# Attention stage of a decoder trunk: TensorE's order pinned as traced, projections dealt anew, look-ahead of seven tiles

## Chip, cores and metric

One core of one Trainium2 chip. The metric is device time in microseconds of one execution, median of 3 runs.

## The reference

One layer: a modulated RMSNorm, one input projection, an RWKV-7 group (8 heads x 64) and a stick-breaking attention group (8 heads x 64), gates, an output projection and a final norm, for 2048 tokens of 1024 features in float32. The change touches the attention group and the projections that run beside it:

```python
def block(args):
    q_blk, idx = args
    z = einsum('bhqd,bhkd->bhqk', q_blk, k) * scale
    log_1m = where(mask, log_sigmoid(-z), 0.0)
    after = cumsum(log_1m, axis=3, reverse=True) - log_1m
    attn = where(mask, exp(log_sigmoid(z) + after), 0.0)
    return einsum('bhqk,bhkd->bhqd', attn, v)
```

So each weight is sigmoid(z) times the product of sigmoid(-z) over all later keys, then the weights are summed with V.

## The kernel before

Three stages follow each other: an early one (modulation, normed input, first projections), the attention stage, and the RWKV stage with the output projection. The first two share a scheduler, which sets each engine's order from a simulated timeline of its own; RWKV has another.

The attention stage has 16 steps n = 4j + b: head pair j of four, block b of four of 512 tokens. Step b has 8(b + 1) tiles of 128 queries by up to 512 keys, since only earlier keys count. `seq` lists all tiles. For one tile, `scores` makes two TensorE matmuls into a PSUM tile `z` (high and low part of the queries in `qt` against the keys in `kt`), ScalarE takes two sigmoids (`u`, `s`), VectorE scans `u` from the last key to the first, and GpSimd multiplies `s` by it. `turn` transposes one key block of the four tiles of a group into the PSUM tile `tr`; ScalarE copies it (`ah`) and VectorE takes the difference (`al`), which together hold the full precision. `weigh` makes two matmuls of V with `ah` and `al`, summed in the one PSUM tile `av`. `attend` calls `scores` for the tile LEAD places ahead, then `turn`, then `weigh` for the tile LAG places behind. At a step's end `finish` transposes the result (`otp`), norms it and stores it in DRAM.

Beside it, `fill` makes the projections that later steps need: K, Q and V of a step (`proj_k`, `proj_q`, `proj_v`) and the gates (`proj_g`, kinds g and r, one for each block), each 24 matmuls of 512 columns (V: 96 of 128 columns) into a PSUM tile `mm`, from weights split by `w_split`. After a Q projection ScalarE copies (L419), VectorE takes the low part (L420) and three DMAs spread it over the partitions (L422 to L424); the third writes what the first two read, so it comes after them. `combine` fetches a finished output, transposes it and multiplies it by its gate. `_merge` interleaves `attend` and `fill` by their estimated work (`fill_work`), and this gives the traced order; the scheduler then chooses its own.

PSUM has eight banks: one `mm`, three `z`, two `tr` (also used by `otp`, `wtp` of `w_split` and `combine`), one `av`, one for a mask. A projection is bound to the last sum traced before it (`pace`) from step 12 on.

Of the kernel before, what the change touches and what calls it, by code (L numbers as in the profile page):

```python
# [18 lines left out]
P = 128  # L19
D = 1024  # L20
KB = D // P
# [67 lines left out]
def trunk(nc, a, out):  # L89
# [22 lines left out]

    NM = [1, 3, 2]
    early = [True]

    def mm_ps(name="mm"):
        if early[0]:
            return z_ps(name)
        return pp.tile([P, TB], F32, tag="mm", bufs=NM[0], name=name)

# [95 lines left out]
    for e in range(2):  # L216
        mrow = [f("mrow") for f in ((z_ps, z_ps) if e == 0 else (z_ps, av_ps))]
        for k in range(KB):
            ad = ada_rows(e, k)
            for i in range(2):  # L220
                PE.matmul(mrow[i][0:1], cact[:, k:k + 1], ad[:, i * TB:(i + 1) * TB], start=k == 0, stop=k == KB - 1)
        if e == 0:
            load_x(0)
        modr = xp_.tile([P, D], F32, tag="macc", bufs=2, name="modr")
        for i in range(2):
            A.activation(out=modr[0:1, i * TB:(i + 1) * TB], in_=mrow[i][0:1], func=AF.Copy)
        for m in range(8):
            PE.matmul(mod[:, 8 * e + m:8 * e + m + 1], modr[0:1, m * P:(m + 1) * P], ones[0:1, 0:1],
                      start=True, stop=True)
# [95 lines left out]
    def w_split(kind, j):  # L325
# [4 lines left out]
        dg = wl.rearrange("p k c -> p (k c)")[:, 0:2 * P].bitcast(F32)  # L330
        A.activation(out=dg, in_=ident, func=AF.Copy, scale=m1)
        tp = tr_ps("wtp")
        PE.matmul(tp[:, 0:P], ones, dg, start=True, stop=True)
# [28 lines left out]

    pace = [None]

    def inproj(w, b, name):
        wh, wl = w[0], w[1]
        ps = mm_ps(name)
        for k in range(KB):
            with tc.issue_after(pace[0]) if pace[0] is not None else nullcontext():
                PE.matmul(ps, wh[:, k], hth[b][:, k], start=k == 0, stop=False)  # L370
            PE.matmul(ps, wh[:, k], htl[b][:, k], start=False, stop=False)  # L371
            PE.matmul(ps, wl[:, k], hth[b][:, k], start=False, stop=k == KB - 1)  # L372
            yield 0.65
        return ps

    def inproj_tok(w, b, name):
        wh, wl = w[0], w[1]
        ps = mm_ps(name)
        for i in range(4):
            t = slice(i * P, (i + 1) * P)  # L380
            for k in range(KB):
                PE.matmul(ps[:, t], hth[b][:, k, t], wh[:, k], start=k == 0, stop=False)
                PE.matmul(ps[:, t], hth[b][:, k, t], wl[:, k], start=False, stop=False)
                PE.matmul(ps[:, t], htl[b][:, k, t], wh[:, k], start=False, stop=k == KB - 1)
                if k % 4 == 3:
                    yield 0.65
# [74 lines left out]
    def combine(j, b, pool):  # L461
# [9 lines left out]
        DMA.dma_start(out=sg, in_=ydram[4 + j][b])  # L471
        yield 0.45
        tp = tr_ps()
# [6 lines left out]

    NS, NU, LEAD, LAG = 8, 5, 5, 3

# [12 lines left out]
    def scores(n, i, sb):  # L495
# [9 lines left out]
        z = z_ps()  # L505
        PE.matmul(z[:, 0:nk], qt[:, h, 0, qs], kt[:, h, 0:nk], start=True, stop=False)  # L506
        PE.matmul(z[:, 0:nk], qt[:, h, 1, qs], kt[:, h, 0:nk], start=False, stop=True)  # L507
        u = sb.tile([P, TB + 1], F32, tag="u", bufs=NU, name="u")
# [19 lines left out]
    def turn(n, i, sb):  # L528
# [5 lines left out]
        for q in range(q0, 4):  # L534
            PE.transpose(tp[:, q * P:(q + 1) * P], att[gi, q][:, ks * P:(ks + 1) * P], ident)  # L535
        r = slice(q0 * P, TB)
# [6 lines left out]
    def weigh(sb, n, i, ah, al, r):  # L543
# [8 lines left out]
        vs = vst[NB * j + kb][:, ks, h].rearrange("p l d -> p (l d)")  # L552
        PE.matmul(av[:, r], vs, ah[:, r], start=first, stop=False, skip_group_check=True)  # L553
        ins = PE.matmul(av[:, r], vs, al[:, r], start=False, stop=last, skip_group_check=True)  # L554
        if n >= 12:
            pace[0] = ins.ins
        if last:
# [29 lines left out]
    def attend(n, sb):  # L587

        p0 = seq.index((n, 0))
        p1 = p0 + 8 * (n % NB + 1)  # L590
        ahead = LEAD if n % NB else 0
        if n % NB == 1 or n == 0:
            for p in range(p0, p0 + LEAD):
                yield scores(*seq[p], sb)
        for p in range(p0, p1):
            if p + LEAD < min(p1 + ahead, len(seq)):
                yield scores(*seq[p + LEAD], sb)
# [39 lines left out]
    _merge((make_hs(*range(2, NB)), 3.6 * (NB - 2)), (proj_qkv(1), 15.6), (w_split("g", 0), 0.3))  # L637
    gate_row()
    xctx.close()
    cz = [zero1]  # L640
# [6 lines left out]
    def fill(n, sb):  # L647

        j, b = divmod(n, NB)
        end = j == NB - 1  # L650
        if n < 2:
            m = n + 2
        else:
            m = n + 1 if 2 < n < NST - 1 else None
        new = b == 3 and not end
        if b == 0 and j > 0:
            yield from w_split("g", j)
        if b == 2:
            yield from w_split("r", j)
            w_load("z" if end else "k", 0 if end else j + 1)  # L660
        if b == 3:
            yield from w_split("z" if end else "k", 0 if end else j + 1)
            w_load("rk" if end else "q", 0 if end else j + 1)
        gates = [("g", 0)], [("g", 1)], [("g", 2), ("g", 3), ("r", 0)], [("r", 1), ("r", 2), ("r", 3)]
        gates = [proj_g(kind, j, gb, sb) for kind, gb in gates[b]]
        if m is not None:
            yield from proj_k(m)
            if new:
                yield from gates.pop(0)
                yield from w_split("q", j + 1)  # L670
                w_load("v", j + 1)
            yield from proj_q(m)
            if new:
                yield from gates.pop(0)
                yield from w_split("v", j + 1)
                w_load("g", j + 1)
            yield from proj_v(m)
        if j > 0:
            yield from combine(j - 1, b, sb)
        if n == NST - 1:  # L680
            for i in range(4):
                yield from proj_z(i, sb)
                if gates:
                    yield from gates.pop(0)
                if i < 3:
                    yield from w_split(("rk", "rr", "rv")[i], 0)
                if i < 2:
                    w_load(("rr", "rv")[i], 0)
        for g in gates:
            yield from g  # L690
        if b == 1:
            w_load("r", j)

    def fill_work(n):
        b = n % NB
        if n == NST - 1:
            return 5.2 * 7 + 1.5
        return 5.2 * ((4, 4, 6, 6)[b] - 3 * (n == 2)) + 0.9 * (n > 3) + (0.2, 0, 0.2, 0.6)[b]

    dts = []  # L700
    early[0] = False
    with tc.tile_pool(name="sb", bufs=2) as sb:
# [7 lines left out]
        for n in range(NST):  # L710
            b = n % NB
            _merge((attend(n, sb), 8.6 + 10.48 * b), (fill(n, sb), fill_work(n)))
            if n == 1:
# [3 lines left out]
                for i in range(2):  # L717
                    dts.append(dram(f"dt{i}", [2, 2, 8, 65, 64]))
                    for m in range(2):
                        for h in range(2):  # L720
                            DMA.dma_start(out=dts[i][m, h].rearrange("c s t -> s c t")[0:64],
                                          in_=zeros[0:64].rearrange("p (c d) -> p c d", c=8))
    sbk.close()
    pace[0] = None

# [610 lines left out]
```

## Time and profile before

| | |
|---|---|
| median of 3 runs | 1914.78 us (1912.62 to 1915.76) |
| profiled execution | 1910.53 us |
| its span, first to last instruction | 1908.8 us |
| attention stage in it | 129.8 to 1035.8 us |

A row of the timeline gives start, duration, engine, line, operation, what is written from what, shape and count; in brackets the idle time before it and who ended it. Matmuls are pipelined, and a record lasts longer than the distance to the next start. The stretch view gives busy time of each engine, with counts, the granted share of TensorE's clock, and DMA share and rate.

### The profile page before, as it was taken

What the parts mean: (1) busy time and instruction counts of PE and PEld (TensorE: products, weight loads), DVE (VectorE), ACT (ScalarE), POOL (GpSimd) and SP (SyncE); (2) the same over time, 40 slices, a digit from 0 to 9 for tenths busy, and PEclk for the clock granted to TensorE, in tenths of its full rate; (3) what the DMA queues carried; (4) which work ended last, traced back from release to release, by engine and by line L of the source; (5) the groups of instructions that cost most, each with busy time, mean ns of one, the idle gap of its engine ahead of it and who ended that gap; (6) DMA issues with size and microseconds to landing.
All of it is one profiled execution on the core that took longest, in us unless ns stands there. A gap on an engine that the chain in (4) does not pass through costs nothing. (4 is left out here: it accounts for less than half of the span.)

```text
span 1908.8 us, 38922 instructions
## 1 busy us (share of the span) xinstructions
PE 1719.8 (90%) x14880; PEld 1161.5 (61%) x14880; DVE 1348.7 (71%) x2855; ACT 870.0 (46%) x1718; POOL 754.6 (40%) x1106
## 2 busy tenths in 40 slices
PE   7979889999899998999997898898899888989998
PEld 2646556666566665667654455665555565667886
DVE  4876788577776778768775667877877777775542
ACT  2665567366654656546654333323332333422221
POOL 1425466355643646445444223222223232223322
PEclk9889999999999999999998899999999999999999
DMA  8442201222123221132111423222333333236442
GB/s 298 150 116 56 56 26 50 64 64 70 37 56 81 67 56 42 51 92 67 45 50 56 133 55 83 68 60 74 77 81 81 80 77 107 75 94 179 149 138 89
DMA packets 210408, 159.93 MB, mean 84 GB/s; under 512 B 113247, under 2 KB 171820, under 8 KB 210222
## 3 DMA queue, kind: packets, MB, share of 16 engines
q1 hardware_dynamic: 209220, 155.31, 29.2%
q8 instruction: 117, 1.92, 0.4%
q10 hardware_dynamic: 1002, 2.13, 0.4%
q14 instruction: 69, 0.57, 0.1%
HBM read 94.48 MB, written 44.04 MB: 73 GB/s over the span
## 5 line engine op out<-in xcount | busy, mean ns | idle before, releaser
L523 POOL TENSOR_TENSOR s<-s,u 128x512 f32<-128x512 f32 (+2 forms) x320 | 305.8, 963 | 216.5 <-ACT s L511 102.0
L540 DVE TENSOR_TENSOR al<-tr,ah 128x512 fp32r<-128x512 f32 (+1 forms) x320 | 187.4, 599 | 96.3 <-ACT ah L539 95.7
L522 DVE TENSOR_TENSOR_SCAN u<-u,dmask 128x512 f32<-128x512 f32 x192 | 240.0, 1268 | 13.0 <-ACT u L510 11.4
L539 ACT ACTIVATE ah<-tr 128x512 fp32r<-128x512 f32 (+1 forms) x320 | 171.7, 553 | 103.7 <-PE tr L535 99.6
L510 ACT ACTIVATE u<-z 128x512 f32<-128x512 f32 (+2 forms) x320 | 173.4, 555 | 73.4 <-PE z L507 49.0
L535 PE MATMUL tr<-kept_ident,s 128*128 128x128 f32 x1088 | 173.5, 279 | 33.1 <-DVE al L540 26.5
L511 ACT ACTIVATE s<-z 128x512 f32<-128x512 f32 (+2 forms) x320 | 166.2, 549 | 53.0 <-PE tr L535 53.0
L535 PEld LDWEIGHTS tr<-kept_ident,s 128*128 128x128 f32 x1088 | 130.3, 143 | 74.9 <-DVE al L540 38.4
L370 PE MATMUL pss<-kept_hh,kept_wh 128*128 128x512 f16 x416 | 161.3, 388 | 8.8 <-PEq L730 8.8
L372 PE MATMUL pss<-kept_hh,kept_wl 128*128 128x512 f16 x416 | 160.9, 387 | 0.0
L371 PE MATMUL pss<-kept_hl,kept_wh 128*128 128x512 f16 x416 | 160.9, 387 | 0.0
L372 PEld LDWEIGHTS <-kept_wl 128*128 128x128 f16 x928 | 93.2, 100 | 104.9 <-issue 14.2
L370 PEld LDWEIGHTS <-kept_wh 128*128 128x128 f16 x928 | 94.3, 102 | 101.4 <-issue 29.2
L371 PEld LDWEIGHTS <-kept_wh 128*128 128x128 f16 x928 | 93.0, 100 | 94.8 <-issue 25.0
L506 PE MATMUL z<-kt,qt 128*128 128x512 f32 (+2 forms) x320 | 132.1, 417 | 9.5 <-issue 3.7
L553 PE MATMUL av<-ah,vt 128*128 128x512 f32 (+1 forms) x320 | 136.5, 427 | 3.9 <-DVE o L564 2.3
L554 PE MATMUL av<-al,vt 128*128 128x512 f32 (+1 forms) x320 | 136.0, 426 | 0.2 <-DVE al L540 0.2
L507 PE MATMUL z<-kt,qt 128*128 128x512 f32 (+2 forms) x320 | 117.5, 371 | 0.0
L519 DVE TENSOR_TENSOR_SCAN u<-u,dmask 128x128 f32<-128x128 f32 (+3 forms) x128 | 107.3, 867 | 11.6 <-ACT u L510 6.6
L370 PE MATMUL psg<-kept_hh,kept_wh 128*128 128x512 f16 x256 | 99.1, 387 | 10.9 <-DVE klo L434 4.8
L1274 PE MATMUL po<-kept_woh,kept_yh 128*128 128x512 f32 x256 | 102.3, 400 | 0.0
L1275 PE MATMUL po<-kept_wol,kept_yh 128*128 128x512 f32 x256 | 101.5, 397 | 0.0
(296 smaller groups left out, 4146.1 us busy)
## 6 DMA issues: line engine op xcount, KB each, us to landing
kept_raw<-in_w_in SPq DMA_DIRECT2D x29, 512.0 KB, 4.3
ad<-in_ada_w SPq DMA_DIRECT2D x24, 512.0 KB, 5.6
qt<-qt SPq DMA_DIRECT2D x48, 256.0 KB, 3.3
xt<-in_x SPq DMA_DIRECT2D x16, 512.0 KB, 5.1
y<-sg SPq DMA_DIRECT2D x32, 256.0 KB, 2.3
t<-dt SPq DMA_DIRECT2D x64, 128.0 KB, 3.2
xr<-in_x SPq DMA_DIRECT2D x16, 512.0 KB, 3.6
out<-xr SPq DMA_DIRECT2D x16, 512.0 KB, 2.6
```

The costliest lines, as they stand in the source:

```text
L370: PE.matmul(ps, wh[:, k], hth[b][:, k], start=k == 0, stop=False)
L371: PE.matmul(ps, wh[:, k], htl[b][:, k], start=False, stop=False)
L372: PE.matmul(ps, wl[:, k], hth[b][:, k], start=False, stop=k == KB - 1)
L510: A.activation(out=u[:, 0:nk], in_=z[:, 0:nk], func=AF.Sigmoid, scale=-0.125)
L511: A.activation(out=s[:, 0:nk], in_=z[:, 0:nk], func=AF.Sigmoid, scale=0.125)
L522: V.tensor_tensor_scan(out=ur, data0=ur, data1=mr, initial=u[:, nk:nk + 1], op0=ALU.mult, op1=ALU.bypass)
L523: G.tensor_tensor(out=s[:, 0:nk], in0=s[:, 0:nk], in1=u[:, 1:nk + 1], op=ALU.mult)
L535: PE.transpose(tp[:, q * P:(q + 1) * P], att[gi, q][:, ks * P:(ks + 1) * P], ident)
L539: A.activation(out=ah[:, r], in_=tp[:, r], func=AF.Copy)
L540: V.tensor_tensor(out=al[:, r], in0=tp[:, r], in1=ah[:, r].bitcast(F32), op=ALU.subtract)
L553: PE.matmul(av[:, r], vs, ah[:, r], start=first, stop=False, skip_group_check=True)
L554: ins = PE.matmul(av[:, r], vs, al[:, r], start=False, stop=last, skip_group_check=True)
```

## The change

TensorE's matmuls of scores, transposes, sums and projections in the attention stage are chained in the order in which they are traced (`pin`, `pinned`). PSUM has two `mm`, two `z`, two `tr` buffers. The look-ahead is seven tiles and goes on over the ends of steps, the sums are one tile behind. `s` and `u` have 11 and 6 buffers. The projections of the four steps of a head pair are dealt 3, 4, 6, 7 (before 4, 4, 6, 6) and in another sequence. `w_split` and `combine` hand over more often.

```diff
-    NM = [1, 3, 2]
-    early = [True]
+    NM = [2, 2, 2]
     def mm_ps(name="mm"):
-        if early[0]:
-            return z_ps(name)
         return pp.tile([P, TB], F32, tag="mm", bufs=NM[0], name=name)
...
-        mrow = [f("mrow") for f in ((z_ps, z_ps) if e == 0 else (z_ps, av_ps))]
+        mrow = [f("mrow") for f in ((z_ps, z_ps) if e == 0 else (mm_ps, mm_ps))]
...
         A.activation(out=dg, in_=ident, func=AF.Copy, scale=m1)
+        yield 0.3
         tp = tr_ps("wtp")
...
-    pace = [None]
+    order = []
+    def pin(ins):
+        order.append(ins.ins)
+    def pinned():
+        for p, i in zip(order, order[1:]):
+            tc.add_manual_dep(i, p.name, mybir.DependencyInfo(mybir.DependencyClass.NoSync,
+                                                              mybir.DependencyReason.DATA), reason="order")
+        order.clear()
...
-            with tc.issue_after(pace[0]) if pace[0] is not None else nullcontext():
-                PE.matmul(ps, wh[:, k], hth[b][:, k], start=k == 0, stop=False)
-            PE.matmul(ps, wh[:, k], htl[b][:, k], start=False, stop=False)
-            PE.matmul(ps, wl[:, k], hth[b][:, k], start=False, stop=k == KB - 1)
+            pin(PE.matmul(ps, wh[:, k], hth[b][:, k], start=k == 0, stop=False))
+            pin(PE.matmul(ps, wh[:, k], htl[b][:, k], start=False, stop=False))
+            pin(PE.matmul(ps, wl[:, k], hth[b][:, k], start=False, stop=k == KB - 1))
...
-        yield 0.45
+        for _ in range(1 if pool is None else 3):
+            yield 0.8
         tp = tr_ps()
...
-    NS, NU, LEAD, LAG = 8, 5, 5, 3
+    NS, NU, LEAD, LAG = 11, 6, 7, 1
...
-        ahead = LEAD if n % NB else 0
-        if n % NB == 1 or n == 0:
+        if n == 0:
             for p in range(p0, p0 + LEAD):
                 yield scores(*seq[p], sb)
         for p in range(p0, p1):
-            if p + LEAD < min(p1 + ahead, len(seq)):
+            if p + LEAD < len(seq):
+                while seq[p + LEAD][0] not in qst:
+                    yield 0.02
                 yield scores(*seq[p + LEAD], sb)
```

The new `fill`, its core:

```python
def g(kind, gb):
    return proj_g(kind, j, gb, sb)
def kqv(m):
    yield from proj_k(m)
    yield from proj_q(m)
    yield from proj_v(m)
if b == 0:
    ...
    yield from kqv(n + 1 if j > 0 else 2)
if b == 1:
    yield from kqv(n + 1 if j > 0 else 3)
    yield from g("g", 2 if j > 0 else 3)
if b == 2:
    ...
    if j > 0:
        yield from kqv(n + 1)
    yield from g("g", 3 if j > 0 else 2)
    yield from g("r", 3)
    yield from g("r", 2)
if b == 3 and not end:
    ...
    yield from g("g", 1)
    ...
    yield from proj_k(n + 1)
    ...
    yield from proj_q(n + 1)
    yield from proj_v(n + 1)
    yield from g("g", 0)
    yield from g("r", 0)
    yield from g("r", 1)
```

The order that results, at two places. First TensorE at the change from step 4 to step 5, before: from the last Q matmuls of step 5 (`psq`) to the start of its V projection (`psv`, 96 matmuls).

```order
L372 MATMUL psq<-kept_hh_510,kept_wl_288 128x512
L553 MATMUL av<-ah,vt 128x512
L554 MATMUL av<-al,vt 128x512
L553 MATMUL av<-ah,vt 128x384
L554 MATMUL av<-al,vt 128x384
L553 MATMUL av<-ah,vt 128x256
L554 MATMUL av<-al,vt 128x256
L535 MATMUL tr<-kept_ident_61,s 128x128 x4
L553 MATMUL av<-ah,vt 128x128
L535 MATMUL tr<-kept_ident_61,s 128x128 x3
L554 MATMUL av<-al,vt 128x128
L382 LDWEIGHTS kept_hh_510
```

Eight sums and seven transposes stand here; the 96 V matmuls and two more transposes follow, and then the first scores of step 5. Now, the same engine, from the end of the twelfth V matmul behind the last Q matmul:

```order
L392 LDWEIGHTS kept_hl_511
L392 MATMUL psv<-kept_wh_313,kept_hl_511 128x128
L515 MATMUL z<-kt,qt 128x128
L516 MATMUL z<-kt,qt 128x128
L544 MATMUL tr<-kept_ident_61,s 128x128 x3
L390 LDWEIGHTS kept_hh_510
L390 MATMUL psv<-kept_wh_313,kept_hh_510 128x128
```

The first scores of step 5 now stand behind 12 V matmuls, with the remaining 84 and three transposes behind them. K and Q of step 5 (48 matmuls) stand ahead, with one pair of sums, one tile's transposes and the `otp` of step 3 among them.

Second, TensorE in the middle of a long step (step 6), before, at the end of one gate projection (`psg`) and the start of the next:

```order
L506 MATMUL z<-kt,qt 128x512
L507 MATMUL z<-kt,qt 128x512
L506 MATMUL z<-kt,qt 128x512
L507 MATMUL z<-kt,qt 128x512
L535 MATMUL tr<-kept_ident_61,s 128x128 x4
L506 MATMUL z<-kt,qt 128x512
L507 MATMUL z<-kt,qt 128x512
L553 MATMUL av<-ah,vt 128x512
L535 MATMUL tr<-kept_ident_61,s 128x128 x3
L554 MATMUL av<-al,vt 128x512
L370 LDWEIGHTS kept_wh_822
L370 MATMUL psg<-kept_hh_1011,kept_wh_822 128x512
```

Here three tiles' scores, two tiles' transposes and a sum stand together, and 14 projection matmuls follow in a row. Now, within a Q projection of step 5:

```order
L515 MATMUL z<-kt,qt 128x512
L516 MATMUL z<-kt,qt 128x512
L378 LDWEIGHTS kept_wh_287
L378 MATMUL psq<-kept_hh_806,kept_wh_287 128x512
L379 LDWEIGHTS kept_wh_287
L379 MATMUL psq<-kept_hl_807,kept_wh_287 128x512
L380 LDWEIGHTS kept_wl_288
L380 MATMUL psq<-kept_hh_806,kept_wl_288 128x512
L544 MATMUL tr<-kept_ident_61,s 128x128 x4
L562 MATMUL av<-ah,vt 128x512
L563 MATMUL av<-al,vt 128x512
```

One tile's scores, three or six projection matmuls, one tile's transposes and the sums of the tile before it now alternate.

## Rows read from the trace of the kernel before

**Rows 1.** Stretch view: steps 4 and 7, then the whole attention stage.

```profile
core 0: us, PE busy (x) PEld busy (x) DVE busy (x) ACT busy (x) POOL busy (x), PEclk, DMA share, GB/s
359.30:389.80 30.50, 28.37 (x216) 19.71 (x214) 16.05 (x27) 14.03 (x33) 11.95 (x24) 0.94 0.30 79
...
495.40:589.50 94.10, 84.67 (x511) 56.59 (x510) 71.82 (x107) 51.96 (x106) 45.68 (x79) 0.97 0.20 57
...
129.80:1035.80 906.00, 833.70 (x5352) 569.63 (x5352) 678.79 (x1007) 535.92 (x1125) 469.72 (x836) 0.98 0.21 56
```

**Rows 2.** Stretch view of line L371 alone, then of L383 alone, attention stage.

```profile
129.80:1035.80 906.00, 189.53 (x496) 48.92 (x496) 0.98 0.21 56
...
129.80:1035.80 906.00, 77.84 (x448) 43.81 (x448) 0.98 0.21 56
```

**Rows 3.** Costliest groups, TensorE: count, busy us, mean ns, idle before and its releasers.

```profile
L535 PE MATMUL tr<-kept_ident,s 128*128 128x128 f32 x1088 | 173.5, 279 | 33.1 <-DVE al L540 26.5
...
L506 PE MATMUL z<-kt,qt 128*128 128x512 f32 (+2 forms) x320 | 132.1, 417 | 9.5 <-issue 3.7
```

**Rows 4.** Timeline of TensorE in step 7: start us, duration, engine, line, operation.

```profile
563.74 0.22 PE L383 MATMUL psv<-kept_wl,kept_hh 128*128 128x128 f16 x1
563.79 0.22 PE L384 MATMUL psv<-kept_wh,kept_hl 128*128 128x128 f16 x1
...
571.05 0.38 PE L372 MATMUL psg<-kept_hh,kept_wl 128*128 128x512 f16 x1
571.26 1.04 PE L535 MATMUL tr<-kept_ident,s 128*128 128x128 f32 x8
572.06 0.47 PE L553 MATMUL av<-ah,vt 128*128 128x512 f32 x1
572.37 0.40 PE L554 MATMUL av<-al,vt 128*128 128x512 f32 x1
572.61 0.39 PE L370 MATMUL psg<-kept_hh,kept_wh 128*128 128x512 f16 x1
...
575.68 0.39 PE L506 MATMUL z<-kt,qt 128*128 128x512 f32 x1
575.91 0.40 PE L507 MATMUL z<-kt,qt 128*128 128x512 f32 x1
576.15 0.39 PE L370 MATMUL psk<-kept_hh,kept_wh 128*128 128x512 f16 x1
```

**Rows 5.** Waits of TensorE, attention stage: who waited for whom, total us, times, longest.

```profile
PE tr L535 <- DVE al L540: 26.5, 27, 2.2
PE psq L370 <- DVE klo L434: 5.2, 3, 1.7
...
PE psg L370 <- DVE klo L434: 4.8, 3, 2.1
PE z L506 <- issue: 3.7, 2, 1.8
...
PE psg L370 <- DVE sg L456: 3.3, 1, 3.3
PE psg L370 <- DVE z L403: 2.6, 1, 2.6
...
PE z L506 <- DMA qt<-qt: 1.9, 1, 1.9
```

**Rows 6.** Timeline of TensorE, step 4 to 5; last, the view of tile `qt`.

```profile
359.91 0.38 PE L372 MATMUL psq<-kept_hh,kept_wl 128*128 128x512 f16 x1
...
370.10 0.30 PE L506 MATMUL z<-kt,qt 128*128 128x128 f32 x1 [1.83 <-issue]
...
DMA to landing us min/median/max: 2.8/3.3/4.5
```

**Rows 7.** Stretch view, five microseconds behind that wait.

```profile
371.00:376.00 5.00, 5.00 (x17) 1.98 (x17) 2.70 (x4) 2.25 (x7) 3.24 (x9) 0.66 0.19 56
```

**Rows 8.** Costliest groups: VectorE's difference and ScalarE's copy.

```profile
L540 DVE TENSOR_TENSOR al<-tr,ah 128x512 fp32r<-128x512 f32 (+1 forms) x320 | 187.4, 599 | 96.3 <-ACT ah L539 95.7
L539 ACT ACTIVATE ah<-tr 128x512 fp32r<-128x512 f32 (+1 forms) x320 | 171.7, 553 | 103.7 <-PE tr L535 99.6
```

More of the change, by code (lines that the diff above doesn't have):

```diff
@@ L381, in inproj_tok @@
             for k in range(KB):
-                PE.matmul(ps[:, t], hth[b][:, k, t], wh[:, k], start=k == 0, stop=False)
-                PE.matmul(ps[:, t], hth[b][:, k, t], wl[:, k], start=False, stop=False)
-                PE.matmul(ps[:, t], htl[b][:, k, t], wh[:, k], start=False, stop=k == KB - 1)
+                pin(PE.matmul(ps[:, t], hth[b][:, k, t], wh[:, k], start=k == 0, stop=False))
+                pin(PE.matmul(ps[:, t], hth[b][:, k, t], wl[:, k], start=False, stop=False))
+                pin(PE.matmul(ps[:, t], htl[b][:, k, t], wh[:, k], start=False, stop=k == KB - 1))
                 if k % 4 == 3:
@@ L505, in scores @@
         z = z_ps()
-        PE.matmul(z[:, 0:nk], qt[:, h, 0, qs], kt[:, h, 0:nk], start=True, stop=False)
-        PE.matmul(z[:, 0:nk], qt[:, h, 1, qs], kt[:, h, 0:nk], start=False, stop=True)
+        pin(PE.matmul(z[:, 0:nk], qt[:, h, 0, qs], kt[:, h, 0:nk], start=True, stop=False))
+        pin(PE.matmul(z[:, 0:nk], qt[:, h, 1, qs], kt[:, h, 0:nk], start=False, stop=True))
         u = sb.tile([P, TB + 1], F32, tag="u", bufs=NU, name="u")
@@ L534, in turn @@
         for q in range(q0, 4):
-            PE.transpose(tp[:, q * P:(q + 1) * P], att[gi, q][:, ks * P:(ks + 1) * P], ident)
+            pin(PE.transpose(tp[:, q * P:(q + 1) * P], att[gi, q][:, ks * P:(ks + 1) * P], ident))
         r = slice(q0 * P, TB)
@@ L552, in weigh @@
         vs = vst[NB * j + kb][:, ks, h].rearrange("p l d -> p (l d)")
[L553 to L556, printed above, removed]
+        pin(PE.matmul(av[:, r], vs, ah[:, r], start=first, stop=False, skip_group_check=True))
+        pin(PE.matmul(av[:, r], vs, al[:, r], start=False, stop=last, skip_group_check=True))
         if last:
@@ L638, in trunk @@
     gate_row()
+    order.clear()
     xctx.close()
@@ L650, in fill @@
         end = j == NB - 1
[L651 to L657, printed above, removed]
+        def g(kind, gb):
+            return proj_g(kind, j, gb, sb)
+        def kqv(m):
+            yield from proj_k(m)
+            yield from proj_q(m)
+            yield from proj_v(m)
+        if b == 0:
+            if j > 0:
+                yield from w_split("g", j)
+            w_load("r", j)
+            yield from kqv(n + 1 if j > 0 else 2)
+        if b == 1:
+            yield from kqv(n + 1 if j > 0 else 3)
+            yield from g("g", 2 if j > 0 else 3)
         if b == 2:
@@ L660, in fill @@
             w_load("z" if end else "k", 0 if end else j + 1)
[L661 to L677, printed above, removed]
+            if j > 0:
+                yield from kqv(n + 1)
@@ new lines, in fill @@
+            yield from g("g", 3 if j > 0 else 2)
+            yield from g("r", 3)
+            yield from g("r", 2)
+        if b == 3 and not end:
+            yield from w_split("k", j + 1)
+            w_load("q", j + 1)
+            yield from g("g", 1)
+            yield from w_split("q", j + 1)
+            w_load("v", j + 1)
+            yield from proj_k(n + 1)
+            yield from w_split("v", j + 1)
+            w_load("g", j + 1)
+            yield from proj_q(n + 1)
[3 more added lines that the diff above has]
+            yield from g("r", 1)
@@ new lines, in fill @@
+        if b == 3 and end:
+            yield from w_split("z", 0)
+            w_load("rk", 0)
+            yield from g("g", 1)
+            yield from proj_z(0, sb)
+            yield from proj_z(1, sb)
+            yield from g("r", 1)
+            yield from w_split("rk", 0)
+            w_load("rr", 0)
+            yield from g("g", 0)
+            yield from g("r", 0)
+            yield from w_split("rr", 0)
+            w_load("rv", 0)
+            yield from proj_z(2, sb)
+            yield from w_split("rv", 0)
+            yield from proj_z(3, sb)
@@ L678, in fill, with fill_work @@
         if j > 0:
             yield from combine(j - 1, b, sb)
+    def fill_work(n):
+        j, b = divmod(n, NB)
         if n == NST - 1:
[L681 to L698, printed above, removed]
+            return 5.2 * 8 + 4.6
+        return 5.2 * ((3, 4, 6, 7)[b] - 3 * (n == 2)) + 2.85 * (j > 0) + (0.5, 0, 0.5, 1.4)[b]
     dts = []
-    early[0] = False
     with tc.tile_pool(name="sb", bufs=2) as sb:
@@ L722, in trunk @@
                                           in_=zeros[0:64].rearrange("p (c d) -> p c d", c=8))
+    pinned()
     sbk.close()
-    pace[0] = None
     HS = [slice(0, 64), slice(64, 128)]
```

## Prediction

> **What bounds the kernel now.** I read the stretch view first, for the attention stage: from the first score matmul to the last finishing transpose, 129.8 to 1035.8 us [rows 1]. TensorE is busy for 833.7 of these 906 us, VectorE for 678.8, so TensorE sets the pace. But a matmul's record outlasts its place in the pipeline, so I worked out what the stage's matmuls need when they follow each other without a wait. By the timeline [rows 2] a 512-column projection matmul follows the next after 0.21 to 0.22 us (0.216 taken), a 128-column one after 0.055, a pair of scores takes 0.47 us (575.68 to 576.15), and eight transposes with a pair of sums 1.35 us (571.26 to 572.61), so a transpose 0.11. The counts: 3 x 496 wide and 3 x 448 narrow projection matmuls [rows 3], one line of three standing for all three; 1088 transposes and 320 pairs of scores [rows 4], as many pairs of sums, and 112 transposes of finish and combine. A diagonal group's four tiles have 128 to 512 columns, so an average pair over the 192 full and 128 diagonal tiles has 435 columns and takes 0.40 us. Sum: 321 + 74 + 132 + 128 + 128 + 3 for small ones = 786 us.
>
> So 120 of 906 us are not work at rate. They fall in three: 72.3 us of recorded idleness (906 - 833.7); 18 us of half clock (granted mean 0.98 [rows 1]); and 30 us left, waits so short that a record's tail covers them.
>
> The waits of TensorE [rows 5] say what the idleness is. 26.5 us: a transpose waits for VectorE's difference `al`, which frees the transposes' PSUM buffer. 5.2 + 4.8 + 3.3 + 2.6 = 15.9 us: a projection waits for the eviction of the one before it, since there is one `mm` buffer. 3.7 + 1.9 us: three times scores wait for a new `qt`. About 25 us are small ones that I leave as they are.
>
> **The change, part by part.** No instruction is added on any engine; the work is the same 786 us, dealt differently. So only the waits count.
>
> *Two `mm` buffers, two for `z`.* A projection has 24 matmuls, 24 x 0.216 = 5.2 us, and the eviction before it has that long. The 15.9 us go: **-15.9**. What covers them is the other buffer; a projection alone in a row would still be covered. The third `z` buffer is lost; in the new order a score tile stands at least a tile's work behind the one whose buffer it takes, for all but a few, and I cost it at nothing.
>
> *Order pinned, sums one tile behind.* Between a tile's transposes and its sums ScalarE's copy (0.55 us) and VectorE's difference (0.60 us) must run [rows 6], 1.15 us and the hand-overs. I counted the TensorE work that stands between, tile by tile in both orders, at the rates of [rows 2]. Under 1.8 us of it stands there for 77 of 320 tiles before and 37 now; the missing time sums to 40 us before and 16 now. For the reuse of a transposes' buffer the sums at 1.8 us are 23 and 15. Both fall, the first by three fifths, because the old order set whole projections in one block and attention tiles close together. I take three fifths off the 26.5 us and off the 30 us of short waits: **-15.9** and **-18**. Bounds: nothing (if the queues of ScalarE and VectorE make these waits, not TensorE's order) and all of 56.5.
>
> *Seven tiles ahead, over step ends.* Before, look-ahead stopped at the end of each b = 0 step; now it goes on, and this has a price. Step 4 (8 and 12 alike) has eight tiles and a look-ahead of seven, so at its second tile the scores of step 5 are due, whose K and Q are only then projected. The trace shows how long a `qt` takes: the last Q matmul begins at 359.91, ends at 360.29, and the first score starts at 370.10 [rows 7], 9.8 us. In between lie the copy, the difference and two DMAs in sequence, 3.3 us each at the median. The order of before has 7.5 us of TensorE work there: 96 narrow matmuls (5.3), nine transposes (1.0), eight sums (1.2); TensorE waited 1.8 to 1.9 us. The new order has twelve narrow matmuls, 0.7 us, so TensorE stands for 9.8 - 0.7 = 9.1 us, three times, with the turned tiles, the V projection and the sums queued behind the score matmul. 27.3 instead of 5.6 (3.7 + 1.9): **+21.7**. On SyncE one store of step 3's output now stands between the second and the third `qt` DMA; its data come from transposes 2.8 us ahead of the last Q matmul, so I cost it at nothing, for the third DMA waits over 3 us for the first anyway. In steps 6, 10 and 14 the cover is 7.2 us; at most 2.6 us each, and other waits stretch it: **+3**, bounds 0 and 7.8.
>
> The Trainium skill (SBUF — State Buffer, The DMA setup-cost knee) puts a DMA at some 2 us and its bytes at 436 GB/s, by estimate 2.6 us for these 256 KB. By it the chain would be 1.4 us shorter and the sum 4 us lower, at 1884; the trace's 3.3 us is used.
>
> *Projections dealt 3, 4, 6, 7.* Step 7 lasted 94.1 us with 84.7 of TensorE records and 71.8 of VectorE work [rows 1]. It gets one projection more, 5.2 us, whose eviction is one more pass of VectorE over 128x512, some 0.6 us by the like of it [rows 6]: still TensorE's step. Step 4 (30.5 us) gives that projection away, but the wait above takes the room. Net nothing.
>
> *Clock.* After the 1.83 us wait at 370.10 the granted clock fell to 1.2 GHz: mean 0.66 from 371 to 376, 5 x 0.34 = 1.7 us lost [rows 8]. The three long waits bring one or two such stretches each, 2.5 us taken, 7.5 in all; of today's 18 I keep 8.5, since half the waits that precede them go: **-2**, bounds -12 and +5. The Trainium skill (TensorE: Matmul & The Clock Gate, Why this matters for your kernels) says an idle gap between bursts returns the clock to half rate; the row agrees. By that rule alone, three falls added and none taken away, the term would be +5 and the time 1895.
>
> The rest (early projections through `mm` buffers, the `yield` before `wtp`, `combine`'s two more yields, `proj_g` in another sequence) moves single instructions that wait for nothing new; the RWKV stage has its own scheduler and keeps its order.
>
> Sum: -15.9 - 15.9 - 18 - 2 + 21.7 + 3 = -27.1. The profiled execution took 1910.5 us (1908.8 of span, 1.7 around it), 4.3 below the median of 1914.8. So 1883.4 for such an execution, **1888 us** for the median, 1.4% faster.
>
> **Rivals.** *All short waits go.* For it: 277 of 320 sums now have 2 us or more of TensorE work between them and their transposes, 232 before, and VectorE has idle time. Against it: VectorE's scans and evictions share a queue with the differences. Price: -15.9 - 26.5 - 30 - 12 + 21.7 = -62.7, 1852 us.
>
> *Slower: the three `qt` waits decide.* If the short waits come from the queues of ScalarE and VectorE, TensorE's order doesn't shorten them, and only the two `mm` buffers gain: -15.9 + 21.7 + 3 + 5 (clock) = +13.8, 1929 us. It decides if the 56.5 us of short waits shrink by less than 14, a quarter. For it: the wait is certain from the order and its chain is measured. Against it: the counted distances.
>
> *A draw.* VectorE, at 71.8 of step 7's 94.1 us, would be at some 73 of 84, and its fuller queue would give back most of what the order gains: a fifth off the short waits, 11 us. Price: -15.9 - 11 - 2 + 24.7 = -4.2, 1911 us.
>
> **How the numbers follow.** The forecast, 1872 to 1904, has 0.56; all short waits gone 0.17; slower 0.15; the draw 0.12. A measurement of this kernel tells about 0.2% (3.8 us) from no change. Faster by more: 0.56 + 0.17 and a third of the draw, 0.77; within it 0.08, from the draw; slower 0.15. The range, 1856 to 1918, leaves out the last of the second case and most of the third.
>
> **What would show it.** Right: waits of a projection for `klo` or `sg` near zero; waits of a transpose for `al` near 11 us; three waits of `z` for `qt` of about 9 us, ahead of the first scores of steps 5, 9 and 13; the stage at about 880 us; the RWKV stage as long as before. Wrong: `z` waits of 2 us (the chain is covered after all); `al` waits of 25 us or more (the slower rival); VectorE without gaps in steps 3, 7 and 11 (the draw); or a difference after the attention stage, which I costed at nothing.

## The result, and the profile after

The changed kernel takes **1963.54 us** (median of 4 runs, 1961.82 to 1967.52) against 1915.27 us for the kernel before in the same series: ratio 1.0252 [1.0228, 1.0275], 2.5% slower. The forecast was 1888 us, and the range, up to 1918, missed it by 45 us. The profiled execution took 1967.52 us, its span is 1965.6.

(The recorded prediction numbers its groups of rows otherwise than the section ahead of it: its rows 2, 3, 4, 6, 7 and 8 are the groups 4, 2, 3, 8, 6 and 7 there; 1 and 5 agree. Below, the groups' own numbers are used.)

I read in the order of [rows 1] and [rows 5]. First the stretch view of the changed kernel: the attention stage, step 4, the stretch around the wait for `qt`, the 5.2 us behind it, step 7.

```profile
core 0: us, PE busy (x) PEld busy (x) DVE busy (x) ACT busy (x) POOL busy (x), PEclk, DMA share, GB/s
105.70:1087.20 981.50, 864.07 (x5433) 576.51 (x5432) 707.99 (x1031) 569.93 (x1145) 475.76 (x838) 0.96 0.21 56
356.40:393.80 37.40, 23.21 (x183) 17.65 (x182) 17.63 (x27) 14.22 (x32) 13.18 (x25) 0.82 0.31 79
362.00:376.00 14.00, 5.17 (x38) 4.61 (x39) 2.19 (x7) 1.34 (x4) 3.46 (x6) 0.51 0.42 95
...
370.80:376.00 5.20, 5.17 (x38) 4.61 (x39) 1.04 (x2) 0.94 (x3) 0.74 (x3) 0.52 0.11 32
...
506.60:601.60 95.00, 87.99 (x527) 57.29 (x526) 74.02 (x108) 57.15 (x113) 48.11 (x83) 0.98 0.18 50
```

The stage ends at 1087.2 instead of 1035.8, so 51.4 us later; behind it the RWKV stage takes 878.4 us (873.0 before). TensorE is idle for 117.4 us of the stage, 72.3 before; but the first score matmul now starts at 105.7 instead of 129.8, so this stage holds more of the early work. A table of the steps' ends (start of the last finishing transpose) shows where the loss comes from:

```
end of step      3      4      5      6      7     11     15
before       359.3  389.8  436.3  495.4  589.5  817.6  1035.8
after        356.4  393.8  438.2  506.6  601.6  845.7  1087.2
later by      -2.9    4.0    1.9   11.2   12.1   28.1    51.4
```

Up to step 3 nothing is lost. Each later head pair loses 15 to 23 us, and each b = 0 step lasts 7 to 9 us longer than before: step 4 took 30.5 us [rows 1], now 37.4. From the end of step 3 to the end of the stage the work is all but the same (4090 and 4101 matmul records), so this stretch compares like with like (before, then now):

```profile
359.30:1035.80 676.50, 630.28 (x4090) 429.84 (x4088) 505.42 (x755) 396.74 (x827) 345.73 (x602) 0.98 0.22 59
...
356.40:1087.20 730.80, 641.94 (x4101) 429.90 (x4100) 514.12 (x756) 414.26 (x829) 346.82 (x602) 0.97 0.21 56
```

TensorE is idle there for 88.8 us instead of 46.2, and the clock takes some 22 us instead of 14. What is left without idleness and clock is 620 us and was 617, the same within the rounding of the clock's two digits.

The waits of TensorE in the stage, against [rows 5]:

```profile
PE z L515 <- DMA qt<-qt: 36.3, 6, 11.4
PE av L563 <- DVE al L549: 23.6, 34, 2.3
PE wtp L331 <- ACT kept_wl L328: 18.4, 7, 3.9
PE otp L579 <- DVE o L571: 7.9, 13, 1.4
PE tr L544 <- DVE al L549: 7.7, 13, 0.9
PE av L562 <- DVE o L571: 7.2, 6, 2.0
...
PE z L515 <- ACT s L520: 2.3, 1, 2.3
```

The row of the kernel before for `al` on the second sums, which [rows 5] does not have:

```profile
PE av L554 <- DVE al L540: 0.2, 1, 0.2
```

The projections' waits for `klo` and `sg` are gone. The waits for `al` are not fewer, they have moved: 26.5 us on transposes and 0.2 on sums before, now 7.7 and 23.6. Scores wait 36.3 us for `qt`, and `wtp`, the weight split's small matmul, which was no row of the stage before, waits 18.4 us for ScalarE. The wait at the end of step 4, in the timeline, against [rows 6]:

```profile
359.08 0.38 PE L380 MATMUL psq<-kept_hh,kept_wl 128*128 128x512 f16 x1
...
359.50 0.69 ACT L427 ACTIVATE qt<-psq,kept_uns 128x512 fp32r<-128x512 f32 x1 [2.21 <-PE psq L380]
...
360.41 1.22 DVE L316 TENSOR_REDUCE wm<-kept_raw 128x8 f32<-128x1024 f32 x1 [4.48 <-DMA kept_raw<-in_w_in]
...
362.41 0.74 DVE L428 SCALAR_TENSOR_TENSOR qt<-psq,kept_uns,qt 128x512 fp32r<-128x512 f32 x1
...
363.17 0.46 SPq L430 DMA_DIRECT2D qt<-qt  x1
...
367.87 0.46 SPq L432 DMA_DIRECT2D qt<-qt  x1
...
370.83 0.45 PE L515 MATMUL z<-kt,qt 128*128 128x128 f32 x1 [10.71 <-DMA qt<-qt]
```

From the end of the last Q matmul (359.46) to the first score it is 11.4 us, where the prediction had 9.8. VectorE stands 4.48 us waiting for a weight load (`wm`), and the low part is queued behind it, so it starts at 362.41, 2.95 us after that end. While TensorE stands the granted clock falls to its lower level (1.2 GHz), and the 5.2 us after the restart run at 0.52; in [rows 7] the 5 us behind the shorter wait ran at 0.66.

The two groups of [rows 8] hardly differ; a difference of VectorE takes 593 ns (599 before), so it is not slower, but waited for at another place:

```profile
L549 DVE TENSOR_TENSOR al<-tr,ah 128x512 fp32r<-128x512 f32 (+1 forms) x320 | 189.8, 593 | 17.4 <-ACT ah L548 16.6
L548 ACT ACTIVATE ah<-tr 128x512 fp32r<-128x512 f32 (+1 forms) x320 | 171.9, 537 | 31.8 <-PE tr L544 31.4
```

### The profile page after: what moved, and what is told of

It is laid out like the page before. It is cut to its first block, busy times and chain, and to the rows that moved or that the text cites. A ratio compares the mean times of both kernels' runs of the same rounds, so it can differ in the third digit from the quotient of the medians.

```text
span 1965.6 us, 39082 instructions
## 1 busy us (share of the span) xinstructions
PE 1735.6 (88%) x14880; PEld 1161.1 (59%) x14880; DVE 1361.3 (69%) x2855; ACT 891.9 (45%) x1718; POOL 757.3 (39%) x1106
## 5 line engine op out<-in xcount | busy, mean ns | idle before, releaser
L531 DVE TENSOR_TENSOR_SCAN u<-u,dmask 128x512 f32<-128x512 f32 x192 | 245.0, 1276 | 79.1 <-ACT u L519 61.9
L528 DVE TENSOR_TENSOR_SCAN u<-u,dmask 128x128 f32<-128x128 f32 (+3 forms) x128 | 111.9, 877 | 108.5 <-ACT u L519 100.4
L515 PE MATMUL z<-kt,qt 128*128 128x512 f32 (+2 forms) x320 | 150.6, 471 | 38.6 <-DMA qt<-qt 36.3
L562 PE MATMUL av<-ah,vt 128*128 128x512 f32 (+1 forms) x320 | 161.0, 503 | 7.6 <-DVE o L571 7.2
L544 PEld LDWEIGHTS tr<-kept_ident,s 128*128 128x128 f32 x1088 | 133.5, 143 | 47.7 <-issue 6.8
L563 PE MATMUL av<-al,vt 128*128 128x512 f32 (+1 forms) x320 | 123.1, 385 | 23.9 <-DVE al L549 23.6
L516 PE MATMUL z<-kt,qt 128*128 128x512 f32 (+2 forms) x320 | 118.6, 371 | 0.0
L1300 PE MATMUL po<-kept_woh,kept_yl 128*128 128x512 f32 x256 | 101.6, 397 | 0.0
```

What stands on the lines that cost most here:

```text
L531: V.tensor_tensor_scan(out=ur, data0=ur, data1=mr, initial=u[:, nk:nk + 1], op0=ALU.mult, op1=ALU.bypass)
L544: pin(PE.transpose(tp[:, q * P:(q + 1) * P], att[gi, q][:, ks * P:(ks + 1) * P], ident))
L562: pin(PE.matmul(av[:, r], vs, ah[:, r], start=first, stop=False, skip_group_check=True))
```

## The experiments

Theory at the start: the three `qt` waits with their clock are most of the loss. Rivals: the pins, the deal, or one tile behind. All ratios are to the kernel before; 0.1 percentage points are 1.9 us.

**e1_stop**: look-ahead stops at b = 0 steps, as before.

```diff
-        if n == 0:
+        ahead = LEAD if n % NB else 0
+        if n % NB == 1 or n == 0:
...
-            if p + LEAD < len(seq):
-                while seq[p + LEAD][0] not in qst:
-                    yield 0.02
+            if p + LEAD < min(p1 + ahead, len(seq)):
```

> The changed kernel with the look-ahead stopped at the end of each b = 0 step and started afresh in the next, as before; pinned order, deal and sums one tile behind stay. 7.0 us of TensorE work then stands between the last Q matmul of steps 4, 8, 12 and the first score (0.7 us in the changed kernel). Theory (the three qt waits of 10.4 to 11.4 us and the half clock they leave are most of the loss): waits of 3 to 4.5 us each, 20 us of waiting and some 15 us of clock less: 1920 to 1935 us. Rival A (the loss is in pinned order and short waits on VectorE's difference): 1950 or more, the waits shrink but the idleness comes back as waits of seven scores in a row for ScalarE.

1931.72 us, 1.0082 [1.0055, 1.0110]. The look-ahead over step ends costs 1.7 points, 33 us. Of the `z` waits for `qt` one of 0.9 us is left, but the kernel is still slower than before; the other waits stay:

```profile
PE wtp L331 <- ACT kept_wl L328: 18.9, 7, 4.5
PE av L563 <- DVE al L549: 18.0, 28, 1.9
PE otp L579 <- DVE o L571: 12.4, 16, 1.8
PE av L562 <- DVE o L571: 10.6, 9, 2.7
```

**e2_cover_v**, **e8_rload**, **e17_gload**: three edits to the `qt` wait alone.

```diff
-                while seq[p + LEAD][0] not in qst:
+                while seq[p + LEAD][0] not in vst:
```

> The changed kernel with one word edited: the scores of a new step wait in the trace until its V projection is there too (vst for qst), so that 5.3 us of narrow matmuls stand between Q and the first score of steps 5, 9, 13 instead of 0.7. Theory: the qt chain keeps its length, 11.4 us, so each of the three waits falls from 10.8 to some 6.2 us: 14 us less, with a part of the clock back 14 to 20: 1943 to 1950 us. Rival B (the wait is not the transfer but whatever is behind it on TensorE): no change, 1960 to 1967.

1941.82 us, 1.0127 [1.0082, 1.0172], with waits of 5.83, 6.14 and 6.46 us: the chain keeps its length, and work put behind it shortens the wait by as much. The time fell by more than the waits did.

```diff
         if b == 0:
-            w_load("r", j)
...
             yield from g("g", 2 if j > 0 else 3)
+            w_load("r", j)
```

> The changed kernel with the load of the r weights moved back from the start of the b = 0 step to the end of the b = 1 step. Theory: in the changed kernel VectorE stands 4.5 us (360.41) in wm, waiting for that load, with the low part of qt queued behind it, so the low part starts 2.95 us after the Q projection's end; without it the low part starts after some 1.0 to 1.4 us, and each of the three waits shrinks by 1.5 to 2.5 us: 5 to 10 us less, 1953 to 1959. Rival B: the DMAs' own time decides and the low part is not what z waits for last: within 3 us of 1963.5.

1963.05 us, 1.0242 [1.0206, 1.0278]: no difference, waits of 10.44 to 11.42 us. `wm` still stands 4.19 us ahead of the low part: I had moved the wrong load, it is that of the g weights. So:

```diff
         if b == 0:
+            yield from kqv(n + 1 if j > 0 else 2)
+            if j > 0:
+                w_load("g", j)
+        if b == 1:
             if j > 0:
                 yield from w_split("g", j)
-            w_load("r", j)
-            yield from kqv(n + 1 if j > 0 else 2)
-        if b == 1:
...
             yield from g("g", 2 if j > 0 else 3)
+            w_load("r", j)
...
             yield from w_split("v", j + 1)
-            w_load("g", j + 1)
```

> The changed kernel with the load of the g weights moved from step 3's end behind the V projection of the b = 0 step, its split to the start of the b = 1 step and the r load to that step's end. In the changed kernel and in e8_rload VectorE stands 4.2 to 4.5 us in wm, waiting for the g weights, just when the Q projection of steps 4, 8, 12 ends, and the low part of qt starts 2.5 to 3.6 us after that end. Theory: without it the low part starts 0.8 to 1.5 us after the end, the three waits fall from 10.4 to 11.4 to 8.1 to 9.3 us: 5 to 10 us less, 1953 to 1959. Rival (the transfers are late for a reason of their own): within 3 us of 1963.5.

The timeline of this run at the same place:

```profile
355.04 0.69 ACT L427 ACTIVATE qt<-psq,kept_uns 128x512 fp32r<-128x512 f32 x1 [2.21 <-PE psq L380]
355.76 0.75 DVE L428 SCALAR_TENSOR_TENSOR qt<-psq,kept_uns,qt 128x512 fp32r<-128x512 f32 x1 [0.89 <-ACT qt L427]
...
364.25 0.45 PE L515 MATMUL z<-kt,qt 128*128 128x128 f32 x1 [8.58 <-issue]
```

The low part follows the copy at once, and the three waits are 8.49 to 8.60 us: so VectorE's standing for the weights was the 2 us above. But 1966.45 us, 1.0282 [1.0256, 1.0308], no gain: steps 5, 9 and 13 now last 47.7 to 47.8 us (44.3 to 44.5 in the changed kernel). The `z` wait for the next `qt` that stands in them is 2.3 to 2.5 us (1.2 to 1.4), and the granted clock of step 5 is 0.96 (1.00). The time was right on the rival's side, the mechanism on the theory's.

**e3_lag3**: the four numbers of before.

```diff
-    NS, NU, LEAD, LAG = 11, 6, 7, 1
+    NS, NU, LEAD, LAG = 8, 5, 5, 3
```

> The changed kernel with the numbers of before: five tiles ahead, sums three tiles behind (8 s, 5 u buffers). Theory (the waits on VectorE's difference, 23.6 us on second sums and 7.7 on transposes, come from sums only one tile behind): those on sums fall under 5 us, those on transposes rise to at most 15; the three qt waits stay at 10 to 11 us (again 0.7 us of work covers them): 10 to 18 us less, 1945 to 1954. Rival C (VectorE's and ScalarE's queues make these waits, wherever the sums stand): the waits only move back to the transposes, 1960 to 1967.

1948.50 us, 1.0172 [1.0126, 1.0218], 15 us less. Sums that wait for `al` are no row of the list any more; transposes wait for it instead, and finishing transposes for `o` (7.9 us in the changed kernel):

```profile
PE tr L544 <- DVE al L549: 14.3, 17, 1.7
PE otp L579 <- DVE o L571: 13.2, 13, 1.7
```

But the three `qt` waits are 8.1 to 8.8 us, not 10 to 11, so only a part of the 15 us is the sums'.

**e6_mm2**: the other end of the ladder, the kernel before with one line edited.

```diff
-    NM = [1, 3, 2]
+    NM = [2, 2, 2]
```

> The kernel before with one line edited: PSUM buffers 2, 2, 2 (mm, z, tr) in place of 1, 3, 2. Everything else (its own order, deal, look-ahead, lag) stays. Theory (as the prediction has it: a second mm buffer takes away the 15.9 us in which a projection waits for the eviction of the one before it): 1898 to 1905. Rival D (those waits only stand in for others: VectorE's and ScalarE's queues are then late at the next transposes or scores, and the lost third z buffer costs): 1911 to 1922.

**1885.75 us**, 0.9837 [0.9792, 0.9882]: 31 us less (22 to 40 by the interval), twice what the prediction gave it, below the span of either theory and below both kernels. Its stage in the stretch view and its waits:

```profile
132.10:1008.00 875.90, 830.27 (x5346) 555.19 (x5344) 677.33 (x1008) 544.46 (x1129) 474.46 (x836) 0.99 0.21 58
```

```profile
PE tr L535 <- DVE al L540: 24.4, 33, 1.6
PE av L553 <- DVE o L564: 3.8, 9, 1.0
PE tr L476 <- DMA ol<-odram: 2.3, 1, 2.3
```

TensorE's idleness falls from 72.3 to 45.6 us: the 15.9 us of the projections, 4.6 of the 5.6 us of scores for `qt`, and some of `otp` and scores; the clock goes from 0.98 to 0.99. Only the waits for `al` stay (24.4).

**e7_pin_mm2**, **e12_pin_att**, **e16_pin_proj** pin that kernel's matmuls as the change does: all, only scores, transposes and sums, only projections. **e18_nopace** is their control.

```diff
-        if n >= 12:
-            pace[0] = ins.ins
```

> The run e6_mm2 with TensorE's attention order pinned as in the change (the pacing of projections in the last four steps goes with it); deal, look-ahead and lag of before. Theory (pinned order gives no shorter waits, and puts the weight split's small matmul, which waits for ScalarE, in front of pinned work): 5 to 15 us above e6_mm2. Rival E (the prediction's: even order takes away short waits): 10 to 25 us below e6_mm2. The difference of the two runs is the price of pinning alone.

> The run e7_pin_mm2 with only scores, transposes and sums pinned; projections go free. Theory (pinned projections standing in the traced order right behind their weights' split make the 100 us between e6_mm2 and e7_pin_mm2: the waits for ScalarE's copy wh are 59 us there): these waits vanish, 1890 to 1910. Rival (pinned attention tiles are as bad): 1940 or more.

> The run e7_pin_mm2 with only the projections pinned; scores, transposes and sums go free. Pins on the attention tiles alone cost 46 us over e6_mm2 (e12_pin_att), on both 100. Theory (a projection that stands in a fixed order waits for its weights' split, and free attention tiles can fill that): 1890 to 1925. Rival (the fixed order of projections is the worse half by itself): 1930 to 1960.

> The run e6_mm2 without the pacing of the last four steps' projections (the pinned runs lack it too, so this is their control). Theory (pacing only sets where the last steps' projections stand): within 5 us of 1885.8, and pins alone stay at 95 us or more. Rival (the pacing makes part of what was put down to pins): 1892 or more.

Control 1889.41 us, 0.9866 [0.9844, 0.9889]; projections pinned 1896.98, 0.9898 [0.9871, 0.9926]; attention pinned 1932.02, 1.0078 [1.0055, 1.0101]; both 1986.18, 1.0360 [1.0318, 1.0403]. So pins alone cost 0.3, 2.1 and 4.9 points: 6 us (within the intervals), 41 and 95 us. My theory on e7_pin_mm2 (5 to 15 us) was far off. With free projections (e12_pin_att) the waits for `kept_wh` fell as expected, from 59.4 to 3.8 us, but the time did not come down to 1910; the theories on e16_pin_proj and the control held. I read it so, and no run shows it by itself: either half leaves the scheduler something to move into a gap, both leave little. The waits of e7_pin_mm2, and one of them in the timeline:

```profile
PE otp L579 <- DVE o L571: 21.8, 15, 2.9
PE psk L379 <- ACT kept_wh L348: 21.2, 3, 7.3
PE psq L379 <- ACT kept_wh L348: 19.5, 3, 6.9
PE psv L391 <- ACT kept_wh L348: 13.7, 3, 7.0
PE tr L544 <- DVE al L549: 11.6, 16, 1.7
```

```profile
518.45 0.28 DVE L336 TENSOR_REDUCE mx<-wtp 128x1 f32<-128x128 f32 x1
...
519.30 1.27 DVE L531 TENSOR_TENSOR_SCAN u<-u,dmask 128x512 f32<-128x512 f32 x1
...
521.95 1.90 POOL L347 TENSOR_TENSOR kept_raw<-kept_raw,rkw 128x1024 f32<-128x1024 f32 x1
...
523.87 1.06 ACT L348 ACTIVATE kept_wh<-kept_raw 128x1024 f16<-128x1024 f32 x1 [4.72 <-POOL kept_raw L347]
...
524.98 0.61 PE L379 MATMUL psk<-kept_hh,kept_wh 128*128 128x512 f16 x1 [6.92 <-ACT kept_wh L348]
```

In the traced order a projection follows its weights' split. The split runs over VectorE (its small steps behind a scan of 1.27 us), GpSimd and ScalarE, and TensorE stands through all of it.

**e9_deal** and **e5_stop_lag3**: the change's deal and sequence, its early phase and yields, with before's numbers and look-ahead; free, and pinned. Both carry the edits of e1_stop and e3_lag3; e9_deal also:

```diff
-    pinned()
+    order.clear()
```

> The run e5_stop_lag3 without the pins: the scheduler's own order, PSUM buffers 2, 2, 2, look-ahead and lag of before, but the deal 3, 4, 6, 7 and the small yields of the change. It differs from e6_mm2 (1885.8) in the deal. Theory (the deal 3, 4, 6, 7 is there to keep other work between a weight split and its projection, which only a pinned order needs; a scheduler does that itself): 1885 to 1900. Rival (the deal itself costs, as the last step with eight projections after the third-last tile): 1910 to 1930.

> The run e1_stop with five tiles ahead and sums three tiles behind, as before; only pinned order, PSUM buffers 2, 2, 2, the deal 3, 4, 6, 7 and the small yields of the change remain. It differs from e7_pin_mm2 in the deal, from e1_stop in the two numbers. Theory (in the changed kernel one tile behind costs 10 to 15 us, as e3_lag3 showed 15): 1917 to 1923. Rival (with the qt waits gone the numbers matter no more): within 4 of e1_stop's 1931.7.

Free 1909.45 us, 0.9953 [0.9929, 0.9977]; pinned 1925.85, 1.0052 [1.0030, 1.0073]. Against e18_nopace the deal costs 0.9 points in a free order. Against e7_pin_mm2 it saves 3.1 points in a pinned one: it sets other projections between a split and its own, and the waits for `kept_wh` are gone from the list. From e9_deal to e5_stop_lag3 the pins cost 1.0 points. From there to e1_stop the numbers cost 0.3, within the intervals. Both came out outside the theory's span, e9_deal 9 us above it and e5_stop_lag3 3. Two rows of e5_stop_lag3, and one of e9_deal, where nothing is pinned:

```profile
PE otp L579 <- DVE o L571: 20.0, 16, 2.7
PE tr L544 <- DVE al L549: 17.3, 21, 1.8
```

```profile
PE wtp L331 <- ACT kept_wl L328: 16.5, 6, 9.1
```

**e4_nopin**, **e13_after_pin_att**: the whole change without pins, and with only attention pinned. **e10_nums**: e6_mm2 with the change's four numbers.

> The changed kernel without the pins: the scheduler orders TensorE's work by its own times, all else as in the change. The order built this way has 7.5 to 10 us of work between the last Q matmul of steps 4, 8, 12 and the first score of the next step. Theory (the three qt waits make the loss, and pinning makes the qt waits by keeping V behind the scores): 1920 to 1935. Rival F (the loss is in seven tiles ahead and one behind, in whatever order): 1950 or more.

> The changed kernel with only scores, transposes and sums pinned; projections go free. In the order built so, 11.5 to 13.5 us of work stand between the last Q matmul of steps 4, 8, 12 and the next step's first score. Theory (V kept behind the scores by the pins makes the three qt waits): they vanish, 1963.5 falls to 1920 to 1938, about where e1_stop and e4_nopin stand. Rival: the waits come back at another operation, 1950 or more.

> The run e6_mm2 with the change's four numbers: seven tiles ahead, sums one tile behind, 11 s and 6 u buffers; nothing pinned, deal and look-ahead's stop as before. Theory (one tile behind costs 10 to 15 us, as in the pinned runs: e3_lag3 showed 15): 1895 to 1902. Rival (a free order puts other work between transposes and sums, so the numbers cost nothing): 1884 to 1889.

1940.59 us, 1.0130 [1.0081, 1.0180]; 1953.97, 1.0182 [1.0135, 1.0229]; 1899.02, 0.9899 [0.9867, 0.9931]. Without pins one `z` wait for `qt` of 1.2 us is left in the stage, yet the change is still slower than before, 6 us above the theory's span. Free projections alone bring 10 to 13 us, at the edge of the intervals, for sums wait 24.6 us for `al` (23.6 in the changed kernel) and finishing transposes 14.1 us for `o` (7.9): the rival's case. The numbers cost 0.6 points in a free order, as the theory had it, but at the edge of the intervals. Two rows of e10_nums show that the numbers alone move the wait for `al` from transposes (24.4 us in e6_mm2) to second sums (0.2 there):

```profile
PE av L554 <- DVE al L540: 24.4, 31, 4.1
...
PE tr L535 <- DVE al L540: 5.3, 7, 1.7
```

**e15_wtp**: the changed kernel with `wtp` four yields behind its diagonal. **e14_early**: e6_mm2 with the change's early phase.

```diff
-        yield 0.3
+        for _ in range(4):
+            yield 0.6
         tp = tr_ps("wtp")
```

> The changed kernel with four yields of 0.6 in place of one of 0.3 between ScalarE's diagonal and the small matmul wtp of a weight split, so that attention tiles stand between them in the traced order. Theory (the 18.4 us in which wtp waits for ScalarE come from the pinned order around it): those waits fall under 5 us and the clock falls at 273, 290, 533, 778 go: 12 to 20 us less, 1944 to 1952. Rival (the tiles in between wait for the same ScalarE, which itself waits for the weights' load): the waits come back at sums, 1957 to 1966.

> The run e6_mm2 with the change's early phase: projections and the rows of the modulation go through the two mm buffers from the start (the flag early is gone). Theory (runs with that early phase end step 0 at 163 to 168 us of the profile, e6_mm2 at 170.4): 2 to 7 us below e6_mm2's 1885.8, 1879 to 1884. Rival (the scheduler's order of the later steps shifts with it, and the head start is lost): 1884 to 1892.

1972.03 us, 1.0287 [1.0259, 1.0314]: `wtp` waits 9.7 us instead of 18.4, but finishing transposes 15.7 (7.9) and the next transposes 8.3 for `combine`; the waits moved, as the rival said, though not to sums, and the time is 6 us above the rival's span. e14_early: 1889.05 us, 0.9865 [0.9839, 0.9890], no different from e6_mm2 and inside its rival's span.

## Why the prediction was wrong

The runs form a ladder in which neighbours differ by one part, or by parts that belong together. Each step is the difference of two ratios, times 1915.3 us; it holds for this order of the parts:

```
part                                      ratio   step us   prediction's term
PSUM buffers 2, 2, 2      (e6_mm2)       0.9837     -31      -16
pacing gone               (e18_nopace)   0.9866      +6        0   unclear
deal, early phase, yields (e9_deal)      0.9953     +17        0
pins                      (e5_stop_lag3) 1.0052     +19   }  -34
seven ahead, one behind   (e1_stop)      1.0082      +6   }        unclear
look-ahead over step ends (the change)   1.0252     +33      +25
clock, by itself                                     in these  -2
sum                                                 +48      -27
```

- **Two `mm` buffers: right, and too small.** The 15.9 us went; about as much again went with them, 4.6 us of scores' waits for `qt` and a part of the clock's falls among it. That these went because projections no longer stood late is my reading.
- **"I take three fifths off the 26.5 us and off the 30 us of short waits": the step that failed.** The three fifths came from a count of the work between a tile's transposes and its sums (40 us missing before, 16 now). But before the change the sums waited only 0.2 us for `al`; the 26.5 us stood on transposes, for which the same count fell by a third, from 23 to 15. And the four numbers, sums one tile behind among them, brought waits of their own: transposes fell to 7.7 us, sums rose to 23.6, together 31.3. e10_nums, without a pin, shows the same move, and with the numbers of before (e3_lag3) the sums' row is gone. Of the 30 us of short waits nothing went, by the 617 and 620 us above. The waits for `al` are shortest where all is pinned and sums stand three behind (11.6 us in e7_pin_mm2, 14.3 in e3_lag3, 17.3 in e5_stop_lag3), and there finishing transposes wait 21.8, 13.2 and 20.0 us for `o` instead (5.1 before). I took pinning for a better order and gave it no price. Its price is that what waits holds everything traced behind it: 95 us on before's deal, 19 us on the new one. With the numbers this step is 59 us off, of the 75 us between -27 and +48.
- **Look-ahead over step ends: right mechanism in the pinned order, 8 us short.** The order gave 0.7 us of cover, as said, but the chain was 11.4 us, not 9.8, because VectorE stood for a weight load ahead of the low part (without it, in e17_gload, 9.2 us, from 355.00 to 364.25). The three long waits are 32.5 us (27.3 predicted); those of steps 6, 10 and 14 are 1.2 to 1.4 each, 4 in all for +3. In a free order the `qt` waits are gone, yet the numbers and the look-ahead together cost 1.8 points, 34 us, from e9_deal to e4_nopin (2.0 points, 38 us, with the pins). Finishing transposes wait 13.8 us for `o` in e4_nopin and 1.4 in e9_deal; the rest of that price stays open, so the 33 us are the price of the look-ahead behind pins only. The DMAs were not the cause, as the view of the tile `qt` shows (against the last line of [rows 6]):

```profile
DMA to landing us min/median/max: 2.8/2.9/6.9
```

  A median of 2.9 us lies between the 3.3 us that I used and the 2.6 us that stand in the prediction as an estimate by the Trainium skill (SBUF — State Buffer, The DMA setup-cost knee); none of these copies landed in less than 2.8.
- **Deal "net nothing": wrong in both directions.** It costs 17 us where the order is free and saves 59 where it is pinned. It suits the pins, and I judged it by steps 4 and 7 alone. e9_deal ends steps 3, 7, 11 and 15 later than e18_nopace by 12, 19, 22 and 26 us, and its `wtp` waits 16.5 us for ScalarE, 9.13 of them in the last step, where e18_nopace has no such wait. How much of the 17 us this is stays open.
- **Clock: the falls right, the recovery wrong.** The stretches behind the three long waits ran at 0.52, 0.50 and 0.70 over 5.2 to 5.3 us, 6.7 us lost for the 7.5 put down. The Trainium skill's rule (TensorE: Matmul & The Clock Gate, Why this matters for your kernels), that an idle gap between bursts returns the clock to half rate, agrees with 0.51 over 362 to 376. What I let go, half of the old falls, did not go: over the stretch of equal work the mean is 0.97, 0.98 before.
- **`wtp`: put at nothing.** The prediction has it among instructions "that wait for nothing new". It waits 18.4 us for ScalarE, which waits for the weights' maximum. The pins do not make this wait, for e9_deal has 16.5 us of it without a pin and e7_pin_mm2, pinned on before's deal, has none in the stage; it came with the deal and its yields. e15_wtp shows that taking half of it away brings nothing as long as the rest stays.
- **The rival "slower"** had the sign, and its condition held: the short waits did not shrink. Its 1929 us lacked the price of the pins and of the deal and were 34 us low.

## What to carry to other kernels

A pinned order is a cost before it is a gain: go through every pinned instruction that waits for a chain over other engines, and price that chain as a stop of the whole engine, unless the traced order itself puts work there. A count of the work ahead of a wait says something only if that wait stands in the trace; look first where it stands. When a change bundles parts, look for the one that takes away a named wait without new order; here one line with a second PSUM buffer was worth 31 us and the rest of the bundle took 80 back. A look-ahead that crosses a stage boundary turns a slack producer into one that is due at once: compare the length of its chain with the work traced behind it.

## What was not expected of the hardware

A strict-order queue shows its price at a distance: a maximum of weights on VectorE that waits 4.48 us for a load delayed a low part by some 2 us, the DMA chain behind it as much, and with it TensorE, whose wait was 10.7 us and 8.6 without that delay. Removing it left the total where it was. And the same pins cost 6 us on projections (within the intervals) and 41 us on attention, but 95 us on both together.
